# Forgetting attention in a two-layer decoder: half-array products for pairs of heads, a written order for TensorE, gate rows without DMAs, and the output projection begun between the last pairs

## The chip, the cores and the metric

The kernel runs on one core of a Trainium2 chip. A core has TensorE (matrix products into psum banks), VectorE, ScalarE and GpSimd for the element-wise work, and SyncE, whose queue issues the weight loads. The metric is the device time of one execution in microseconds (us); lower is better. Each engine works through its own queue in order, and semaphores order the engines against each other.

## The reference

Two layers on an input of 256 tokens by 1024 channels, float32. Layer 0 mixes tokens by native sparse attention, layer 1 by forgetting attention; each is followed by a squared-ReLU MLP of width 4096, with a norm before and after every part. The change touches layer 1's attention:

```python
def fox_attention(q, k, v, logf):            # q, k, v: [1, 256, 16, 64]
    c = jnp.cumsum(logf, axis=1).transpose(0, 2, 1)
    for i in range(nb):                       # two blocks of 128 queries
        lo, hi = i * blk, (i + 1) * blk
        s = jnp.einsum('bqhd,bkhd->bhqk', q[:, lo:hi], k[:, :hi]) * scale
        s = s + c[:, :, lo:hi, None] - c[:, :, None, :hi]
        causal = jnp.arange(lo, hi)[:, None] >= jnp.arange(hi)[None, :]
        p = jax.nn.softmax(jnp.where(causal, s, NEG_INF), axis=-1)
        outs.append(jnp.einsum('bhqk,bkhd->bqhd', p, v[:, :hi]))

def fox_mixer(h, w_in, b_f, w_out):
    q, k, v, fl = jnp.split(h @ w_in, [1024, 2048, 3072], axis=-1)
    logf = jax.nn.log_sigmoid(fl + b_f)
    return fox_attention(q, k, v, logf).reshape(B, T, 1024) @ w_out
```

## The kernel before, in words

**Precision.** A float32 operand is split into a rounded part `hi` and the rest `lo` (`split`, line 114: ScalarE rounds, VectorE subtracts), and a product is the sum hi·hi + lo·hi + hi·lo: three matmuls (`mm3`, line 148). Weights come in pieces of 128x1024 by `load_w` (line 118) on SyncE's queue and are split in the same way; the tiles for them go round through three pools.

**The planner.** The kernel's text is a program order; a planner reorders each engine's instructions by a cost model, ready work first. `tc.keep_in_program_order` pins an instruction to the written place. Tiles come from pools with a fixed number of buffers; `ps_tile(use)` (line 84) gives one of two psum banks of a use: `m`, `s`, `t`, `o` (2 KB per partition each).

**The forgetting layer.** The value projection makes eight blocks of 128 tokens by 256 columns (line 834), with psum uses listed in `VBANKS`; ScalarE evacuates each to `vf` with the token's norm scale (line 838). `token_scales` (line 822) transposes these scales for use along the free axis. Then come eight pairs of heads (line 915). `project` makes q and k of a pair, transposed (128 channels by 256 tokens): per q or k 8 k-steps of `mm3` into one half of an `m` bank, 24 products of 256 columns each. VectorE scales the result to `full` (line 900). Then `qA`, `kA`, `qB` and `kB` are made of it, per head and per q or k: one rounding and one copy on ScalarE (lines 904, 907) and one subtraction on VectorE (905). They stack hi and lo of a head of 64 channels into operands of 128 rows; `kB` has two more rows, the cumulated log gates, which `gates` (line 910) puts there by two DMAs per pair on ScalarE's queue, against rows of ones in `qB`.

`fox_head` (line 853) then takes one head: per block of 128 queries two products (128 rows, and 66 rows) give the scores over 128 or 256 keys in an `s` bank; VectorE adds the mask and finds the minimum (866; signs are turned), ScalarE takes exp with its sum (869), VectorE scales (870, 872); three transposes (875), ScalarE copies them out (877); then the value products in float32 (878, 879), each as two instructions, which write the head's 64 rows of the pair's `o` bank. `fox_pair` (881) splits that bank into `aT`. The planner mixes all this with the projection of later pairs.

**Around it.** `out_proj` (line 656) multiplies `aT` by the output weights into four accumulators (two banks `m` for tokens 0 to 127, two banks `o` for the rest) by `accumulate` (line 620): eight steps i, `go(i, t)` being six products of 512 columns; the second token block lags for the last `DEFER` steps, so that the norm of the first runs beside it. `mlp` (line 670) calls it and then runs the MLP. At most the planner brings its products forward.

Of the kernel before, what the change touches and what calls it, by code (L numbers as in the profile page):

```python
# [8 lines left out]
F32 = mybir.dt.float32  # L9
# [36 lines left out]
NQT = 2  # L46
KBB = 2
SB_B = 3
FB = 2
AHEAD = 1  # L50
VG = 3
CS = 0
VO = (3, 0, 1, 2)
AG = 2
VBANKS = "mmssoomm"
# [13 lines left out]
def kernel(ctx, tc, x_in, norm_g, w_up, w_down, nsa_w_in, nsa_pos, nsa_w1, nsa_w2,  # L69
# [77 lines left out]

    def mm3(ps, lhs, rhs, start, stop):

        pe.matmul(ps, lhs[0], rhs[0], start=start, stop=False)  # L150
        pe.matmul(ps, lhs[1], rhs[0], start=False, stop=False)  # L151
        pe.matmul(ps, lhs[0], rhs[1], start=False, stop=stop)  # L152
# [467 lines left out]
    def accumulate(acc, steps, done):  # L620
# [17 lines left out]

        for i in range(n):
            yield i  # L640
            if i < n - JMAJ:
                go(i, 0)
# [13 lines left out]
    def out_proj(src, w, layer, after):  # L656
        g = load_g(layer, 1)
        acc = [[ps_tile(c) for _ in range(2)] for c in "mo"]
# [3 lines left out]
        def done(t):  # L662
            add_norm(t, acc[t], g)
            return after(t)

        for _ in accumulate(acc, steps, done):
            pass


    def mlp(layer, src, w_out, after):  # L670
# [18 lines left out]
        out_proj(src, w_out, layer, prep)  # L689
# [94 lines left out]
    mlp(0, aT, nsa_w_out[0], to_fox)  # L784
# [11 lines left out]
    cT = [fx1.tile([H, T], R, name=f"cT{i}") for i in range(2)]  # L796

    qBs = [fx1.tile([DH + 2, 2, T], R, name=f"qB{i}") for i in range(NQT)]
    for q in qBs:
        pool.memset(q[DH:DH + 2].bitcast(F32), 1.0)  # L800

    def logf(t, pf):
        a, e, y, m = (stile(H, n) for n in ("fa", "fe", "fy", "fm"))
        z = stile(H, "fz")
# [15 lines left out]
    rT = [fx1.tile([P, T], F32, name=f"rT{j}") for j in range(2)]  # L820

    def token_scales():

        ps = ps_tile("s")
        for t in range(NT):
            rb = fx.tile([P, T], F32, name="full", bufs=FB)[:, 0:P]
            act.activation(rb, ones, AF.Identity, scale=fox_in[t])
            pe.transpose(ps[:, t * P:(t + 1) * P], rb, ident)
        act.copy(rT[1], ps[:, 0:T])
        act.activation(rT[0], ps[:, 0:T], AF.Identity, scale=-SCALE)  # L830
# [3 lines left out]
    for use, (t, i) in zip(VBANKS, vorder):  # L834
# [7 lines left out]
    token_scales()  # L842

    def cumsum():
# [4 lines left out]
        split(cT[0], cT[1], ps[0:H, 0:T])  # L849

    aT = new_hT()

    def fox_head(h, kA, qA, qB, kB, po):
        rows = slice(h % 2 * DH, (h % 2 + 1) * DH)
        ps = ps_tile("s")
        for t in range(NT):
            ts = slice(t * P, (t + 1) * P)
            o, ks = ps[:, t * T:t * T + (t + 1) * P], slice(0, (t + 1) * P)
            pe.matmul(o, qA[:, h % 2, ts], kA[:, h % 2, ks], start=True, stop=False)
            pe.matmul(o, qB[:, h % 2, ts], kB[:, h % 2, ks], start=False, stop=True)  # L860
        psv = ps.rearrange("p (t k) -> p t k", t=NT)
        sb = fx.tile([P, 3, P], F32, name="s_sb", bufs=SB_B)
        s_sb = [sb[:, 0, :], sb[:, 1:3, :].rearrange("p k c -> p (k c)")]
        mx, sums = stile(2, "mx"), stile(2, "sums")
        for t in range(NT):
            dve.tensor_tensor_reduce(out=s_sb[t], in0=psv[:, t, 0:(t + 1) * P], in1=(caus, mask1)[t], scale=1.0,
                                     scalar=HIGH, op0=OP.add, op1=OP.min, accum_out=mx[:, t:t + 1])
        for t in range(NT):
            act.activation(s_sb[t], s_sb[t], AF.Exp, scale=-1.0, bias=mx[:, t:t + 1], accum_out=sums[:, t:t + 1])
# [114 lines left out]
```

## Time and profile before

| | us |
|---|---|
| median of 3 runs (lowest, highest) | 673.53 (672.61, 674.65) |
| the profiled execution's own time | 675.86 |
| its span, first to last instruction | 673.80 |

| busy in the span | TensorE | VectorE | ScalarE | GpSimd |
|---|---|---|---|---|
| us | 652.9 | 454.3 | 394.8 | 36.9 |

The mean granted clock of TensorE is 0.992 of full speed. A row of the timeline gives the start and the duration of one instruction, or of several of one kind merged (x2). Matmuls are pipelined: a recorded duration reaches past the start of the next one, so the cost of a product is read from start to start. Weight loads (LDWEIGHTS, engine PEld) run beside matmuls. Line numbers are those of the kernel before.

### The profile page before, as it was taken

The page shows a single profiled execution, that of the slowest core. Times are in us where ns is not written, and L with a number is a line of the kernel's source. Part 1 is how long each engine was busy: PE and PEld are TensorE (multiplying, and loading weights), DVE is VectorE, ACT ScalarE, POOL GpSimd, SP SyncE. Part 2 cuts the span into 40 slices and gives each one's busy share as a digit, 9 for nine tenths or more (in the row PEclk, how much of TensorE's full clock was granted, in tenths as well). Part 3 has the DMA queues.
Part 4 walks back from the last instruction along what each step waited for, and adds up shares of the span by engine and source line. Part 5 has one row for each costly group of instructions (what it writes and reads, how often), then busy time and mean ns, then how long its engine had stood idle before and what let it go on. Part 6 is the DMA issues. An engine that isn't in the chain of part 4 may idle for free.

```text
span 673.8 us, 10482 instructions
## 1 busy us (share of the span) xinstructions
PE 652.9 (97%) x3889; PEld 567.2 (84%) x3889; DVE 454.3 (67%) x886; ACT 394.8 (59%) x708; POOL 36.9 (5%) x74
## 2 busy tenths in 40 slices
PE   7999999999999999999999899999999999999996
PEld 6998998988788888888889898887878888888884
DVE  5887898764985656556658677777777475566533
ACT  4868587864865454544547568787676355455321
POOL 1000003212100000000003000000010000000000
PEclk8998999999999999999999999999999999999998
DMA  9666852202696655656636732325476567565301
GB/s 308 174 197 189 232 179 90 64 1 71 200 313 201 220 179 168 213 162 207 192 100 185 226 124 93 95 96 165 156 240 204 158 203 219 151 213 173 119 1 62
DMA packets 74867, 110.20 MB, mean 164 GB/s; under 512 B 4728, under 2 KB 60736, under 8 KB 74816
## 3 DMA queue, kind: packets, MB, share of 16 engines
q1 hardware_dynamic: 72336, 105.48, 50.0%
q10 hardware_dynamic: 2480, 4.06, 1.9%
q8 instruction: 30, 0.49, 0.3%
q14 instruction: 21, 0.17, 0.1%
HBM read 108.44 MB, written 1.05 MB: 162 GB/s over the span
## 4 chain that ended last, share of the span: by engine, by line
PE 78%; DMA 7%; DVE 6%; ACT 5%; issue 3%; POOL 1%; SPq 0%; POOLq 0%; DVEq 0%; ACTq 0%
PE ps_m L716 14%; PE ps_m L717 8%; PE ps_m L150 5%; PE ps_m L152 5%; PE ps_m L151 5%; PE ps_o L150 5%; PE ps_o L151 5%; PE ps_o L152 5%; PE ps_s L150 5%; PE ps_s L152 5%; PE ps_s L151 5%; PE ps_o L562 3%; DMA raw<-in_nsa_w_in_dram 2%; DVE lo L116 2%; PE ps_m L719 2%
## 5 line engine op out<-in xcount | busy, mean ns | idle before, releaser
L116 DVE TENSOR_TENSOR lo<-raw,hi 128x1024 fp32r<-128x1024 f32 (+2 forms) x196 | 237.2, 1214 | 114.6 <-ACT hi L115 108.9
L115 ACT CAST hi<-raw 128x1024 fp32r<-128x1024 f32 (+2 forms) x196 | 203.1, 1043 | 126.4 <-DMA raw<-in_mlp_w_up_dram 43.5
L716 PE MATMUL ps_m<-hT,hi 128*128 128x512 f32 x392 | 140.0, 396 | 0.0
L717 PE MATMUL ps_m<-hT,lo 128*128 128x256 f32 x448 | 116.8, 281 | 0.0
L717 PEld LDWEIGHTS ps_m<-hT,lo 128*128 128x128 f32 x448 | 84.5, 189 | 5.0
L716 PEld LDWEIGHTS ps_m<-hT,hi 128*128 128x128 f32 x392 | 73.6, 188 | 16.1
L151 PE MATMUL ps_m<-hi,hT 128*128 128x256 f32 (+3 forms) x252 | 80.4, 319 | 1.1 <-DVE hT L116 1.1
L152 PE MATMUL ps_m<-lo,hT 128*128 128x256 f32 (+3 forms) x252 | 80.3, 319 | 0.7 <-DVE lo L116 0.7
L150 PE MATMUL ps_m<-hi,hT 128*128 128x256 f32 (+3 forms) x252 | 80.9, 322 | 0.0
L151 PEld LDWEIGHTS ps_m<-hi,hT 128*128 128x128 f32 x252 | 48.5, 192 | 4.5 <-DVE hT L116 2.1
L152 PEld LDWEIGHTS ps_m<-lo,hT 128*128 128x128 f32 x252 | 48.4, 192 | 3.5 <-DVE lo L116 1.1
L150 PEld LDWEIGHTS ps_m<-hi,hT 128*128 128x128 f32 x252 | 48.6, 193 | 2.3
L150 PE MATMUL ps_s<-hi,uh 128*128 128x512 f32 x128 | 50.5, 394 | 0.0
L150 PE MATMUL ps_o<-hi,uh 128*128 128x512 f32 x128 | 50.4, 394 | 0.0
L152 PE MATMUL ps_s<-lo,uh 128*128 128x512 f32 x128 | 50.4, 393 | 0.0
L152 PE MATMUL ps_o<-lo,uh 128*128 128x512 f32 x128 | 50.3, 393 | 0.0
L151 PE MATMUL ps_s<-hi,ul 128*128 128x512 f32 x128 | 50.3, 393 | 0.0
L151 PE MATMUL ps_o<-hi,ul 128*128 128x512 f32 x128 | 50.3, 393 | 0.0
L721 ACT COPY second<-ps_m 128x256 f32<-128x256 f32 x56 | 20.7, 370 | 38.8 <-PE ps_m L719 38.6
L150 PE MATMUL ps_m<-hT,hi 128*128 128x256 f32 x128 | 37.6, 294 | 3.6 <-ACT vf L838 2.3
L152 PE MATMUL ps_m<-hT,hi 128*128 128x256 f32 x128 | 37.2, 291 | 0.0
L151 PE MATMUL ps_m<-hT,lo 128*128 128x256 f32 x128 | 36.4, 284 | 0.0
(242 smaller groups left out, 1126.7 us busy)
## 6 DMA issues: line engine op xcount, KB each, us to landing
raw<-in_mlp_w_up_dram SPq DMA_DIRECT2D x64, 512.0 KB, 3.8
raw<-in_mlp_w_down_dram SPq DMA_DIRECT2D x64, 512.0 KB, 4.1
raw<-in_fox_w_in_dram SPq DMA_DIRECT2D x22, 512.0 KB, 3.7
raw<-in_nsa_w_in_dram SPq DMA_DIRECT2D x18, 512.0 KB, 3.5
raw<-in_nsa_cmp_w_dram SPq DMA_DIRECT2D x8, 512.0 KB, 4.6
raw<-in_nsa_w_out_dram SPq DMA_DIRECT2D x8, 512.0 KB, 4.7
raw<-in_fox_w_out_dram SPq DMA_DIRECT2D x8, 512.0 KB, 3.6
gb<-in_norm_g_dram ACTq DMA_DIRECT2D x7, 512.0 KB, 6.6
```

The costliest lines, as they stand in the source:

```text
L115: act.copy(hi, src)
L116: dve.tensor_tensor(out=lo, in0=src, in1=hi.bitcast(F32), op=OP.subtract)
L150: pe.matmul(ps, lhs[0], rhs[0], start=start, stop=False)
L151: pe.matmul(ps, lhs[1], rhs[0], start=False, stop=False)
L152: pe.matmul(ps, lhs[0], rhs[1], start=False, stop=stop)
L562: pe.matmul(pov[:, hh, br, :], pts[:, j * P:(j + 1) * P], vt[:, kt, br, g, :], start=(kt == 0), stop=(kt == t))
L716: pe.matmul(psv, wh[:, fs], hT[2][:, :, k, :], start=k == 0, stop=False)
L717: pe.matmul(psv[:, 0, :], wl[:, fs], hT[0][:, k, :], start=False, stop=False)
L719: pe.matmul(psv, wh[:, fs], hT[2][:, :, k, :], start=False, stop=True)
L721: act.copy(second, psv[:, 1, :])
```

## The change

Heads 2p and 2p+1 are kept in the upper and lower 64 rows of one `hi` and one `lo` tile (q and k side by side, 128x512): one multiplication by `rT`, one split. Per block of queries a head's scores are four products on 64 rows: hi·hi, hi·lo, lo·hi, and a selector column (`sel`, broadcast over 128) times the cumulated gates (`cX`, which holds their hi and lo for both halves); the two heads alternate, each into an `s` bank of its own. So the gate DMAs, `kB` and `qB` are gone. `turn` transposes both heads of a pair in a row; `values` issues both heads' value products in turn. TensorE's order in this part is pinned as written: between the four quarters of the projection of pair p stand the values of pair p-3, the scores of p-1 and the transposes of p-2. After the last projection the first six steps of the output projection for tokens 0 to 127 (`LEAD`) are written between what is left of the pairs. Accumulators are taken when first used. Two of the value blocks use `s` banks in place of `m`, and `token_scales` stands after the fifth block. Elsewhere the text is as it was. The removed functions are printed above.

```diff
-NQT = 2
-KBB = 2
-SB_B = 3
+SB_B = 4
-AHEAD = 1
-CS = 0
-VBANKS = "mmssoomm"
+VBANKS = "mmssooss"
+PB = 4
+LEAD = 6
...
+    as_traced = [False]
+    def queue(ins):
+        if as_traced[0]:
+            tc.keep_in_program_order(ins)
     def mm3(ps, lhs, rhs, start, stop):
-        pe.matmul(ps, lhs[0], rhs[0], start=start, stop=False)
+        queue(pe.matmul(ps, lhs[0], rhs[0], start=start, stop=False))
...
-    def accumulate(acc, steps, done):
+    def accumulate(acc, steps, done, lead=0):
...
+            if callable(acc[t]):
+                acc[t] = acc[t]()
...
+        for i in range(lead):
+            yield i
+            go(i, 0)
         for i in range(n):
             yield i
-            if i < n - JMAJ:
+            if lead <= i < n - JMAJ:
                 go(i, 0)
...
+    sel = fx1.tile([P, H], R, name="sel")
+    for i in range(4):
+        rows = slice(32 * i, 32 * i + 32)
+        pool.tensor_copy(sel[rows], ident[rows, 32 * i:32 * i + H])
+    cX = fx1.tile([P, T], R, name="cX")
+    pool.memset(cX.bitcast(F32), 0.0)
...
-        split(cT[0], cT[1], ps[0:H, 0:T])
+        c = [cX[32 * i:32 * i + H] for i in range(4)]
+        split(c[0], c[1], ps[0:H, 0:T])
+        for i in range(2):
+            act.copy(c[2 + i], c[i].bitcast(F32))
...
     def project(p, ws):
         fs = slice(p % 2 * P, (p % 2 + 1) * P)
         ps = ps_tile("m")
         for j in range(2):
             for k in range(KD):
                 wh, wl = ws[j][k]
+                mm3(ps[:, j * T:(j + 1) * T], (wh[:, fs], wl[:, fs]), (hT[0][:, k, :], hT[1][:, k, :]), k == 0,
+                    k == KD - 1)
+                if k == KD // 2 - 1 or (j == 0 and k == KD - 1):
+                    yield
+        full = fx.tile([P, 2, T], F32, name="full", bufs=FB)
+        dve.tensor_tensor(out=full, in0=ps.rearrange("p (j t) -> p j t", j=2), in1=rT, op=OP.mult)
+        qk[p] = hi, lo = [fx.tile([P, 2, T], R, name=n) for n in ("qk_hi", "qk_lo")]
+        split(hi, lo, full)
+
+    def scores(p):
+        hi, lo = qk.pop(p)
+        ps = [ps_tile("s") for _ in range(2)]
+        for t in range(NT):
+            ts, ks = slice(t * P, (t + 1) * P), slice(0, (t + 1) * P)
+            for i, (q, k) in enumerate(((hi, hi), (hi, lo), (lo, hi), (None, None))):
+                for hh in range(2):
+                    rows = slice(hh * DH, (hh + 1) * DH)
+                    h = 2 * p + hh
+                    queue(pe.matmul(
+                        ps[hh][:, t * T:t * T + (t + 1) * P],
+                        q[rows, 0, ts] if q else sel[rows, h:h + 1].broadcast_to([DH, P]),
+                        k[rows, 1, ks] if k else cX[rows, ks], start=i == 0, stop=i == 3))
...
+    def values(p):
+        po = ps_tile("o")
+        w = pts.pop(p)
+        for kt in range(2):
             for hh in range(2):
+                queue(pe.matmul(po[hh * DH:(hh + 1) * DH, kt * P:T], vf[:, kt, 2 * p + hh, :],
+                                w[hh][:, T:3 * P] if kt else w[hh][:, 0:T], start=kt == 0, stop=kt == 1))
+        split(aT[0][:, p, :], aT[1][:, p, :], po[:, 0:T])
...
+    as_traced[0] = True
     for p in range(KD):
         if p % 2 == 0:
             ws = load_cols(W, p * P, BW), load_cols(W, 1024 + p * P, BW)
+        parts = project(p, ws)
+        next(parts)
+        if p > 2:
+            values(p - 3)
+        next(parts)
+        if p > 0:
+            scores(p - 1)
+        next(parts)
+        if p > 1:
+            turn(p - 2)
+        finish(parts)
+        if p == 0:
             cumsum()
...
+    next(projection)
+    values(KD - 3)
+    fill(1)
+    scores(KD - 1)
+    fill(1)
+    turn(KD - 2)
+    fill(2)
+    values(KD - 2)
+    fill(1)
+    turn(KD - 1)
+    fill(1)
+    values(KD - 1)
+    as_traced[0] = False
```

## Rows read from the trace of the kernel before

**Rows 1.** The page, its first line and its part 4: the span, and the chain of work that ended last, its shares by engine.
```profile
span 673.8 us, 10482 instructions
...
PE 78%; DMA 7%; DVE 6%; ACT 5%; issue 3%; POOL 1%; SPq 0%; POOLq 0%; DVEq 0%; ACTq 0%
```

**Rows 2.** The windows of the value projection and of the attention: from and to, length, then busy us and instructions of TensorE, its weight loads, VectorE, ScalarE, GpSimd, granted clock, DMA share, GB/s.
```profile
360.00:386.00 26.00, 23.65 (x198) 23.41 (x197) 18.87 (x38) 16.50 (x31) 3.44 (x5) 1.00 0.72 223
386.00:470.00 84.00, 81.94 (x587) 70.84 (x587) 63.03 (x186) 66.39 (x173) 0.00 (x0) 1.00 0.35 110
```

**Rows 3.** TensorE's timeline where the attention begins: start us, duration, engine, line, operation, tiles, shape, count, and in brackets the idle time before it.
```profile
382.03 0.38 PE L828 MATMUL ps_s<-ident,full 128*128 128x128 f32 x2
384.76 0.39 PE L150 MATMUL ps_m<-hT,hi 128*128 128x256 f32 x1 [2.35 <-ACT vf L838]
```

**Rows 4.** ScalarE's timeline in the same stretch.
```profile
383.29 1.04 ACT L115 CAST hi<-raw 128x1024 fp32r<-128x1024 f32 x1 [3.10 <-DMA raw<-in_fox_w_in_dram]
384.24 0.47 ACT L838 ACTIVATE vf<-ps_m,rstd 128x256 f32<-128x256 f32 x1
```

**Rows 5.** TensorE's timeline of one head's scores between projection products.
```profile
407.77 0.28 PE L152 MATMUL ps_m<-hT,hi 128*128 128x256 f32 x1
407.89 0.22 PE L859 MATMUL ps_s<-kA,qA 128*128 128x128 f32 x1
407.95 0.27 PE L860 MATMUL ps_s<-kB,qB 66*128 66x128 f32 x1
408.06 0.33 PE L859 MATMUL ps_s<-kA,qA 128*128 128x256 f32 x1
408.23 0.28 PE L860 MATMUL ps_s<-kB,qB 66*128 66x256 f32 x1
408.35 0.29 PE L150 MATMUL ps_m<-hT,hi 128*128 128x256 f32 x1
```

**Rows 6.** TensorE's timeline of one head's value products between projection products.
```profile
401.32 0.28 PE L151 MATMUL ps_m<-hT,lo 128*128 128x256 f32 x1
401.56 0.65 PE L878 MATMUL ps_o<-pts,vf 128*64 128x256 f32 x2
402.04 0.38 PE L879 MATMUL ps_o<-pts,vf 128*64 128x128 f32 x2
402.35 0.39 PE L152 MATMUL ps_m<-hT,hi 128*128 128x256 f32 x1
402.57 0.28 PE L150 MATMUL ps_m<-hT,hi 128*128 128x256 f32 x1
```

**Rows 7.** TensorE's timeline of the last pair's value products, both heads, between products of the output projection.
```profile
468.41 0.40 PE L152 MATMUL ps_m<-lo,hT 128*128 128x512 f32 x1
468.73 0.66 PE L878 MATMUL ps_o<-pts,vf 128*64 128x256 f32 x4
469.21 0.40 PE L879 MATMUL ps_o<-pts,vf 128*64 128x128 f32 x4
469.54 0.50 PE L150 MATMUL ps_o<-hi,hT 128*128 128x512 f32 x1
469.87 0.39 PE L151 MATMUL ps_o<-hi,hT 128*128 128x512 f32 x1
```

**Rows 8.** TensorE's timeline of a pair whose two heads' value products follow each other directly, the first product of each.
```profile
423.84 0.65 PE L878 MATMUL ps_o<-pts,vf 128*64 128x256 f32 x2
...
424.51 0.65 PE L878 MATMUL ps_o<-pts,vf 128*64 128x256 f32 x2
```

**Rows 9.** TensorE's timeline of one head's three transposes among projection products; the products of lines 152 and 150 that start at 412.58 and 412.92 are left out.
```profile
412.32 0.28 PE L151 MATMUL ps_m<-hT,lo 128*128 128x256 f32 x1
412.53 0.30 PE L875 MATMUL ps_t<-ident,s_sb 128*128 128x128 f32 x1
...
412.79 0.38 PE L875 MATMUL ps_t<-ident,s_sb 128*128 128x128 f32 x2
...
413.13 0.28 PE L151 MATMUL ps_m<-hT,lo 128*128 128x256 f32 x1
```

**Rows 10.** TensorE's timeline of eight transposes in a row, in the layer's second norm.
```profile
482.73 1.03 PE L183 MATMUL ps_t<-ident,h 128*128 128x128 f32 x8
483.52 0.48 PE L150 MATMUL ps_o<-hi,hT 128*128 128x512 f32 x1
```

**Rows 11.** Instruction groups of the attention (386 to 470), TensorE's weight loads for the scores: line, engine, operation, tiles, shape, count | busy us, mean ns | idle before them.
```profile
L859 PEld LDWEIGHTS ps_s<-kA,qA 128*128 128x128 f32 x32 | 6.2, 193 | 0.6 <-DVE kA L905 0.6
L860 PEld LDWEIGHTS ps_s<-kB,qB 66*128 66x128 f32 x32 | 6.1, 191 | 0.2 <-issue 0.2
```

**Rows 12.** TensorE's timeline, its longest idle time in the attention.
```profile
442.42 0.38 PE L150 MATMUL ps_m<-hT,hi 128*128 128x256 f32 x1 [0.66 <-DVE full L900]
```

**Rows 13.** Instruction groups of the attention (386 to 470), as in rows 11.
```profile
L116 DVE TENSOR_TENSOR lo<-raw,hi 128x1024 fp32r<-128x1024 f32 x18 | 21.8, 1223 | 2.7 <-ACT hi L115 2.4
...
L904 ACT CAST qA<-full 64x256 fp32r<-64x256 f32 x16 | 6.5, 404 | 1.6 <-DVE cT L116 0.8 <-DVE full L900 0.7
...
L152 PE MATMUL ps_m<-lo,hT 128*128 128x512 f32 x9 | 3.8, 423 | 0.0
```

**Rows 14.** Instruction groups of the whole kernel, each shape by itself: VectorE and ScalarE on 512 columns.
```profile
L116 DVE TENSOR_TENSOR ul<-u,uh 128x512 fp32r<-128x512 f32 x28 | 19.2, 688 | 6.3 <-ACT uh L115 6.2
L115 ACT CAST uh<-u 128x512 fp32r<-128x512 f32 x28 | 17.4, 622 | 27.3 <-DVE u L697 27.3
```

More of the change, by code (lines that the diff above doesn't have):

```diff
@@ L654, in accumulate, with out_proj @@
         finish(done(1) or ())
-    def out_proj(src, w, layer, after):
+    def out_proj(src, w, layer, after, lead=0):
         g = load_g(layer, 1)
-        acc = [[ps_tile(c) for _ in range(2)] for c in "mo"]
+        acc = [lambda c=c: [ps_tile(c) for _ in range(2)] for c in "mo"]
         steps = [(lambda p=p: load_w(w[p * P:(p + 1) * P, :].unsqueeze(1), 1, D), lambda t, p=p: tok(src, p, t))
@@ L663, in done, with mlp @@
             add_norm(t, acc[t], g)
[L664 to L670, printed above, removed]
+            return after[0](t)
+        yield from accumulate(acc, steps, done, lead)
+    def mlp(layer, projection, prepare, after):
         mctx = ExitStack()
@@ L687, in prep @@
             return gen
-        out_proj(src, w_out, layer, prep)
+        prepare.append(prep)
+        finish(projection)
         g3 = load_g(layer, 3)
@@ L841 @@
             logf(t, ps[:, BW:n])
-    token_scales()
+        if j == VG + 1:
+            token_scales()
     def cumsum():
@@ L896, in project @@
             for k in range(KD):
                 wh, wl = ws[j][k]
-                mm3(ps[:, js], (wh[:, fs], wl[:, fs]), (hT[0][:, k, :], hT[1][:, k, :]), k == 0, k == KD - 1)
-            full = fx.tile([P, T], F32, name="full", bufs=FB)
-            dve.tensor_tensor(out=full, in0=ps[:, js], in1=rT[j], op=OP.mult)
-            for hh in range(2):
-                rows, other = (slice(r * DH, (r + 1) * DH) for r in (hh, 1 - hh))
-                top = (qA, kA)[j]
-                act.copy(top[rows, hh, :], full[rows])
-                dve.tensor_tensor(out=qB[0:DH, hh, :] if j == 0 else kA[other, hh, :], in0=full[rows],
-                                  in1=top[rows, hh, :].bitcast(F32), op=OP.subtract)
-                act.copy(qA[other, hh, :] if j == 0 else kB[0:DH, hh, :], full[rows])
@@ new lines, in turn @@
+    def turn(p):
+        pts[p] = []
+        for sb in sbs.pop(p):
+            pt = ps_tile("t")
+            for k in range(3):
+                queue(pe.transpose(pt[:, k * P:(k + 1) * P], sb[:, k, :], ident))
+            pts[p].append(fx.tile([P, 3 * P], F32, name="pts", bufs=PB))
+            act.copy(pts[p][-1], pt[:, 0:3 * P])
+    def values(p):
+        po = ps_tile("o")
+        w = pts.pop(p)
+        for kt in range(2):
+            for hh in range(2):
+                queue(pe.matmul(po[hh * DH:(hh + 1) * DH, kt * P:T], vf[:, kt, 2 * p + hh, :],
+                                w[hh][:, T:3 * P] if kt else w[hh][:, 0:T], start=kt == 0, stop=kt == 1))
+        split(aT[0][:, p, :], aT[1][:, p, :], po[:, 0:T])
@@ L915 @@
+    qk, sbs, pts = {}, {}, {}
+    as_traced[0] = True
     for p in range(KD):
@@ L917, with fill @@
             ws = load_cols(W, p * P, BW), load_cols(W, 1024 + p * P, BW)
-        waiting.append((p, project(p, ws)))
-        if p == CS:
-            cumsum()
-        if p >= AHEAD:
-            i, kq = waiting.pop(0)
-            gates(i, kq[3])
-            fox_pair(i, *kq)
-    for i, kq in waiting:
-        gates(i, kq[3])
-        fox_pair(i, *kq)
+        parts = project(p, ws)
[10 more added lines that the diff above has]
+        if p == 0:
+            cumsum()
+    prepare = []
+    projection = out_proj(aT, fox_w_out[0], 1, prepare, LEAD)
+    def fill(n):
+        for _ in range(n):
+            next(projection)
+    next(projection)
+    values(KD - 3)
[10 more added lines that the diff above has]
+    as_traced[0] = False
     fox_ctx.close()
-    mlp(1, aT, fox_w_out[0], None)
+    mlp(1, projection, prepare, None)
 _INS = ['x', 'norm_g', 'mlp_w_up', 'mlp_w_down', 'nsa_w_in', 'nsa_cmp_pos', 'nsa_cmp_w1', 'nsa_cmp_w2', 'nsa_w_out',
```

83 lines of the change are left out of this document (27 added, 56 removed).

## The prediction

> **What bounds the kernel now.** I read the page first: the span and the chain that ended last [rows 1]. TensorE carries 78% of that chain, and no other engine more than 7%. So an edit is worth what it takes from TensorE's queue, or from TensorE's waits. Then I read the windows of the two stretches that the change touches [rows 2]: the value projection of the forgetting layer (360 to 386) and its attention (386 to 470). The granted clock is 1.00 in both, the 2.4 GHz level, so no stretch has a clock to win. TensorE is busy for 81.94 of 84 us in the attention, VectorE for 63 and ScalarE for 66: these two bound nothing on average, but they hand over what TensorE reads next. In the other stretch TensorE is idle for 2.35 us, nearly all of it in one place [rows 3]. A busy share hides half of this, since a matmul's recorded end runs past the start of the next one. So I price from start to start in the timeline: a 256-column product costs 0.12 us [rows 5] and a 512-column one 0.23 [rows 7].
>
> **The change part by part.** Sums are against the profiled execution, 675.86 us for a span of 673.8; the median of the three runs is 673.53, 2.3 us less, and I carry the difference over.
>
> *The start, -2.5 us.* The two transposes of the token scales start at 382.03, and at 0.10 us each [rows 10] they leave TensorE free at 382.23. The first q product starts at 384.76 [rows 3]. What it waits for is its psum bank: the last two value blocks use the m banks, and their evacuation (vf, 384.24) stands on ScalarE behind a weight cast that waited for its DMA until 383.29 [rows 4]. The new bank list gives these two blocks the s banks, which are next needed by the first scores, some 9 us later. The weights of pair 0 were loaded before those of the cast at 383.29, so I see nothing else that is late there.
>
> *The value products, -6.0 us.* A head on its own costs TensorE 1.01 us: from 401.32 to 402.57 are 1.25 us, in which two projection steps of 0.12 lie [rows 6]. The last pair shows the two heads issued in turn: four and four products from 468.73 on, and the whole visit costs 469.87 - 468.41 less two steps of 0.23, that is 1.00 [rows 7]. Two heads side by side cost what one costs, since each writes 64 of the array's columns. The change writes this order for all eight pairs. Before: pairs 0, 1, 3 and 6 make two visits each (2.02); in pairs 2, 4 and 5 one head directly follows the other, which adds 0.67 [rows 8] (1.68); pair 7 costs 1.00. Together 8.1 + 5.0 + 1.0 = 14.1. After: 8 x 1.01 = 8.1.
>
> *The scores, +2.4 us.* A head's four products now take 0.46 us, 16 heads 7.4 [rows 5]. After, a pair has sixteen products of 64 rows, eight for each head, alternating between upper and lower half of the array and between two banks. No row of this trace has a product on 64 rows beside another. If they run side by side, as the 64-column ones do [rows 7], a pair takes four short and four long steps, twice 0.46 = 0.92: the same as now. To this comes the change of the array's shape. A visit of value products contains 0.48 us for its two long and so about 0.24 for its two short products [rows 6]; the other 0.3 of the 1.01 is what going into and out of half-array products costs. The scores pay none of that now: 0.12 from the product before and 0.12 to the next [rows 5]. So 1.22 per pair, 9.8 in all. Ends: 0.72 per pair (four steps of 0.06 and four of 0.12 and no price for the shape), -1.6 us; sixteen products one behind another (1.84) and the shape, +9.7. I take the value next to [rows 7], as that row shows half-array products.
> The Trainium skill speaks against this part: "TensorEngine Tiling (Array Packing)", Tiling Modes, Key Properties, says that changing the tiling mode drains TensorE. The 0.3 us of [rows 6] agrees with it. Without that rule the scores would cost nothing and the forecast would be 2.4 us lower.
>
> *The transposes, -1.2 us.* A head's three, scattered among projection products, cost 0.45: from 412.32 to 413.13 are 0.81 us, with three steps of 0.12 in it [rows 9]. Six in a row at 0.10 [rows 10], with 0.1 to get back, are 0.7 per pair, 5.6 in all, against 7.2 if all were scattered. Some were not, so 6.8 before; the ends are -0.4 and -1.6.
>
> *TensorE's waits, -1.5 us.* From 384.76 to 469.54 [rows 3, 7] are 84.8 us. In it are 384 projection products (46.1), 27 products of the output projection (nine on each of three lines [rows 13], 6.2), values 14.1, scores 7.4, transposes 6.8, six of the cumulative sum (0.7): 81.3. The 3.5 left are waits, 2.06 of them visible as idle [rows 2], the longest for full [rows 12], that is for the m bank of the projection. In the written order the bank is two pairs deep and that wait goes. What is late next is the chain from the projection's last product to the next scores: full, hi and lo, 0.69 + 0.62 + 0.69 [rows 14], with the 0.28 that a product's record lasts [rows 6] some 2.3 us. Between lie 24 projection products and a value visit, 3.9 us, so 1.6 are left for what stands ahead of these three in the queues of VectorE and ScalarE. At the end, between pair 7's projection and its scores, lie only a value visit and six output products, 2.4: there I expect a wait of 0.5 to 1. I leave 2.0 in all; the ends are 0 and 5.
>
> *At nothing.* The gate rows came by sixteen DMAs of 2 KB from ScalarE's queue; no instruction is shown waiting for them, so their removal gains nothing and the selector product is priced with the scores. ScalarE loses eight casts of 0.40 per pair [rows 13] and gets one of 0.62 [rows 14]; that is cover for the chain above and no time by itself. The output products only move: 36 stand between the pairs' steps where 27 stood, and 60 follow where 69 did. Layer 0 only gets its accumulators later in the text; its order has no reason to change, and I keep 1 us of spread for the planner.
>
> Sum: -2.5 - 6.0 + 2.4 - 1.2 - 1.5 = -8.8, so 667.1 for a profiled execution and 664.7 for the median.
>
> **The rivals.**
> *The half-row products run one behind another.* For: a load of 66 rows takes as long as one of 128 (191 and 193 ns [rows 11]), and the pair has sixteen loads where it had eight. Against: 64-column products do run two by two: the four of one merged row take 0.66 us in [rows 7], the two of one head 0.65 in [rows 6]. Then the scores cost +9.7 and not +2.4: 672.0, no change that can be seen.
> A page's rule bears on it: "TensorE: Matmul & The Clock Gate", LDWEIGHTS, says that a load's time goes by its columns, not its rows, an estimate of 16 x 107 = 1.7 us per pair. The same page, Packing small matmuls, lets loads of different row groups overlap. The loads of [rows 11] agree with the first; no row here shows the second.
> *Slower: the written order waits for the casts in every pair.* TensorE may no longer step around a late operand. If each of the three steps full, hi, lo finds a weight cast ahead of it (1.22 us on VectorE [rows 13], some 1.0 on ScalarE [rows 4]), the chain is 2.3 + 1.2 + 1.0 + 1.2 = 5.7 against 3.9 of cover: 1.8 per pair and 0.2 to refill, 16 in place of my 2.0, and 678.7. It decides from 1.35 us of wait per pair on. For: VectorE is busy 75% of the time with pieces of that size. Against: both engines lose work, and not every pair meets three casts.
> *The shape costs nothing and nothing waits.* 660.3.
> *The start doesn't move,* because the first projection then waits for its weights: 667.2.
>
> **How the numbers follow.** Forecast 0.60, with its own range of 661 to 668.5; side by side fails 0.13; slower 0.10; all free 0.12; start unmoved 0.05. A measurement here tells about 0.3%, 2.0 us, from no change. So faster 0.60 + 0.12 + 0.05 = 0.77, same 0.13, slower 0.10. The range takes in the free case and the one-behind-another case: 660.0 to 672.5.
>
> **What the profile of the changed kernel would show.** The first q product near 382.3. Eight value visits of four and four products, each 1.0 us. Scores as pairs of starts some 15 ns apart, 1.2 us per pair; if starts are 0.11 apart sixteen times, the first rival holds. A TensorE idle total in the attention below 2 us; idle of over 1 us ahead of each pair's scores, ended by lo or hi, means the slower rival. The stage from 382 to the last value product should be 80.6 us with its 36 output products (87.3 now, less 8.8, and nine more products), and a pair some 8.7. I would be wrong at the root if TensorE's total is that much less and the end still doesn't move: then the second MLP's start hung on something else.

## The result, and the profile after

The changed kernel takes 670.35 us (median) beside 673.96 for the kernel before on the same chip: ratio 0.9935, 95% interval 0.9911 to 0.9959, so 2.8 to 6.0 us less. The forecast was 8.8 us less, 664.7; the range (660.0 to 672.5) holds the time, but only about half of the expected gain came, or less. Run again beside the first experiments it took 671.11 against 674.67, ratio 0.9960 (0.9942 to 0.9979). The ratios leave out disturbed executions, and the first profiled one was such (span 2225 us), so "after" below is the profile of that second run, e0_after.

The page of the kernel after, its span and its chain, answers to [rows 1]:

```profile
span 669.1 us, 10502 instructions
...
PE 77%; DMA 7%; DVE 6%; ACT 5%; issue 3%; POOL 1%; SPq 0%; POOLq 0%; DVEq 0%; ACTq 0%
```

TensorE is still the chain, with 77%. The windows answer to [rows 2]: the attention from the first q product on, and then the output projection with the second MLP's norm. The columns are the stretch, its length, busy time and instructions of PE, PEld, DVE, ACT, POOL, then the granted clock, the DMA share and GB/s:

```profile
380.00:465.00 85.00, 82.58 (x676) 73.61 (x675) 58.10 (x160) 48.84 (x121) 0.00 (x0) 0.98 0.44 136
465.00:500.00 35.00, 33.15 (x162) 26.97 (x162) 26.95 (x40) 23.70 (x41) 2.69 (x4) 1.00 0.57 181
```

VectorE and ScalarE are relieved as planned: 58.10 and 48.84 us of work in 85 us where 63.03 and 66.39 stood in 84 [rows 2]. But TensorE is idle for 2.42 us in the attention and 1.85 us behind it, and the clock of the attention is 0.98, where it was 1.00. The timeline of TensorE, kernel after, shows each part of the change in its place; the first two rows answer to [rows 3], the values to [rows 6, 7], the scores to [rows 5], the transposes to [rows 9]:

```profile
380.71 0.28 PE L156 MATMUL ps_s<-lo,hT 128*128 128x256 f32 x1
380.83 0.28 PE L154 MATMUL ps_m<-hT,hi 128*128 128x256 f32 x1
...
407.00 0.28 PE L156 MATMUL ps_m<-hT,hi 128*128 128x256 f32 x1
407.21 0.87 PE L935 MATMUL ps_o<-pts,vf 128*64 128x256 f32 x8
408.01 0.39 PE L154 MATMUL ps_m<-hT,hi 128*128 128x256 f32 x1
408.23 0.28 PE L155 MATMUL ps_m<-hT,lo 128*128 128x256 f32 x1
...
409.43 0.28 PE L156 MATMUL ps_m<-hT,hi 128*128 128x256 f32 x1
409.64 0.33 PE L898 MATMUL ps_s<-qk_hi 64*128 64x128 f32 x2
...
410.75 0.39 PE L154 MATMUL ps_m<-hT,hi 128*128 128x256 f32 x1
410.97 0.28 PE L155 MATMUL ps_m<-hT,lo 128*128 128x256 f32 x1
...
412.15 0.28 PE L156 MATMUL ps_m<-hT,hi 128*128 128x256 f32 x1
412.27 0.82 PE L925 MATMUL ps_t<-ident,s_sb 128*128 128x128 f32 x6
412.85 0.36 PE L154 MATMUL ps_m<-hT,hi 128*128 128x256 f32 x1
413.05 0.28 PE L155 MATMUL ps_m<-hT,lo 128*128 128x256 f32 x1
```

The first q product (ps_m, L154) follows the last value block (ps_s) without a gap, 24.36 us after the first value block's start (356.47); it was 26.78 before. A value visit costs 408.23 - 407.00 less two steps of 0.12: 0.99 us. The scores' rows are pairs of starts ("x2"), eight of them from 409.64 to 410.75, and cost 410.97 - 409.43 less two steps, 1.30. Six transposes cost 0.66 in the same way. A pair without a wait takes 8.7 us (427.63 to 436.30). These are the forecast's own prices, 1.01, 1.22, 0.7 and 8.7. What is not the forecast's is in the view of TensorE's waits (us in total, times, longest), kernel after, from 380 to 500 us:

```profile
PE ps_s L898 <- DVE qk_lo L114: 1.2, 3, 0.4
PE ps_s L898 <- ACT qk_hi L113: 1.1, 1, 1.1
```

The longest of these stands ahead of pair 1's scores; the view's two other entries are the second MLP's hT, further down. Pair 1's scores in the timeline of TensorE, and the stretch in windows of half a microsecond (same columns as above):

```profile
397.40 0.28 PE L156 MATMUL ps_m<-hT,hi 128*128 128x256 f32 x1
398.77 0.33 PE L898 MATMUL ps_s<-qk_hi 64*128 64x128 f32 x2 [1.09 <-ACT qk_hi L113]
399.50 0.33 PE L898 MATMUL ps_s<-qk_lo,qk_hi 64*128 64x128 f32 x2 [0.40 <-DVE qk_lo L114]
...
401.90 0.41 PE L154 MATMUL ps_m<-hT,hi 128*128 128x256 f32 x1
402.12 0.41 PE L155 MATMUL ps_m<-hT,lo 128*128 128x256 f32 x1
```
```profile
401.00:401.50 0.50, 0.50 (x7) 0.50 (x6) 0.50 (x5) 0.50 (x3) 0.00 (x0) 0.86 1.00 410
401.50:402.00 0.50, 0.50 (x4) 0.50 (x4) 0.34 (x3) 0.50 (x3) 0.00 (x0) 0.50 0.65 246
...
404.50:405.00 0.50, 0.50 (x5) 0.50 (x5) 0.00 (x0) 0.04 (x1) 0.00 (x0) 0.72 0.00 0
```

Between 397.40 and 399.50 TensorE starts only the first two of pair 1's scores. And then, with every operand there, the projection's products start 0.21 us apart where they started 0.12 apart: the granted clock has fallen from 2.4 GHz (1.00) to 1.2 GHz (0.50), from about 401.4 to 404.8, 3.4 us in all. The six transposes in that stretch take 1.14 us in place of 0.57, the 24 products behind them 3.53 in place of 3.04, the six ahead 1.23 in place of 0.72: the fall costs 1.6 us, about as much as the waits ahead of it, and no idle column shows it. Who was late is in the timelines of ScalarE and VectorE (in time order, the last figure in brackets is idle time and who ended it):

```profile
386.32 1.05 ACT L113 CAST hi<-raw 128x1024 fp32r<-128x1024 f32 x1 [1.25 <-DMA raw<-in_fox_w_in_dram]
...
390.76 2.00 ACT L113 CAST hi<-raw 128x1024 fp32r<-128x1024 f32 x2
...
396.22 1.98 ACT L113 CAST hi<-raw 128x1024 fp32r<-128x1024 f32 x2
398.11 0.61 ACT L113 CAST qk_hi<-full 128x512 fp32r<-128x512 f32 x1
```
```profile
387.40 1.23 DVE L114 TENSOR_TENSOR lo<-raw,hi 128x1024 fp32r<-128x1024 f32 x1 [1.44 <-ACT hi L113]
...
391.84 2.36 DVE L114 TENSOR_TENSOR lo<-raw,hi 128x1024 fp32r<-128x1024 f32 x2 [1.23 <-ACT hi L113]
394.12 0.28 DVE L909 CUSTOM_DVE_ANT_0 s_sb<-ps_s,cst 128x128 f32<-128x128 f32 x1
...
397.01 0.68 DVE L884 TENSOR_TENSOR full<-ps_m,rT 128x512 f32<-128x512 f32 x1
397.61 1.22 DVE L114 TENSOR_TENSOR lo<-raw,hi 128x1024 fp32r<-128x1024 f32 x1
398.75 0.69 DVE L114 TENSOR_TENSOR qk_lo<-full,qk_hi 128x512 fp32r<-128x512 f32 x1
```

Pair 0's scores end at 391.7, but its first mask operation stands behind two weight lo's (391.84, 2.36 us) until 394.12; full of pair 1 (397.01) stands behind that softmax, qk_hi (398.11) behind two weight casts (396.22, 1.98 us), and qk_lo (398.75) behind qk_hi and one more lo (397.61). The lateness goes back to an earlier cast (386.32) that had waited 1.25 us for its data: its lo (387.40) stands ahead of pair 0's full, which starts at 388.54, 1.8 us behind the end of pair 0's projection (386.75), and qk_hi (389.26) and the two casts at 390.76 follow that. The second MLP's hT, timelines of TensorE, ScalarE and VectorE:

```profile
486.96 0.51 PE L154 MATMUL ps_m<-hi,hT 128*128 128x512 f32 x1 [0.84 <-ACT hT L113]
488.33 0.50 PE L155 MATMUL ps_m<-hi,hT 128*128 128x512 f32 x1 [0.86 <-DVE hT L114]
```
```profile
484.15 1.05 ACT L113 CAST hi<-raw 128x1024 fp32r<-128x1024 f32 x1 [2.77 <-DMA raw<-in_mlp_w_up_dram]
...
486.35 1.05 ACT L113 CAST hT<-ps_t 128x512 fp32r<-128x512 f32 x2
```
```profile
484.96 2.35 DVE L114 TENSOR_TENSOR lo<-raw,hi 128x1024 fp32r<-128x1024 f32 x2
...
487.60 0.67 DVE L114 TENSOR_TENSOR hT<-ps_t,hT 128x512 fp32r<-128x512 f32 x1
```

hT of the second token block comes to ScalarE behind a weight cast that waited 2.77 us for its data and, between the two, the norm's squares of x (from 485.11 on), which come behind that cast too; and to VectorE behind two weight lo's (2.35 us). In the kernel before the one wait here was 0.37 us (for hT, at 493.84).

From first value block to end of span, in three steps read off the timelines, for before, after and the runs told of below (the end of a visit is the start of the next product; the clock's fall is the time at 0.50, summed over half-microsecond windows, without the last 10 us of the span, where the clock falls in every profile):

| run | to the first q product | on to the end of the last value visit (output products in it) | on to the end of the span | time at the lower clock, where |
|---|---|---|---|---|
| before | 26.78 | 84.8 (27) | 204.3 | none |
| e0_after | 24.36 | 83.9 (36) | 204.4 | 3.4, attention |
| e2_planner_order | 24.36 | 80.6 (36) | 204.4 | none |
| e3_old_banks | 25.15 | 81.5 (36) | 206.0 | 3.4, second norm |
| e1_one_after_other | 24.36 | 86.0 (36) | 204.5 | 3.4, attention |
| f1_same_weights | 24.36 | 79.8 (36) | 203.0 | none |
| f2_more_cover | 24.36 | 79.9 (36) | 204.3 | none |
| f3_before_values_only | 26.64 | 83.5 (37) | 205.3 | 3.4, second norm |
| f4_norm_before_casts | 24.36 | 80.9 (36) | 208.4 | 6.8, second MLP |
| g1_norm_one_cast | 24.36 | 81.5 (36) | 203.7 | none |
| g2_cover_again | 24.36 | 79.6 (36) | 204.3 | none |
| g3_cover_and_norm | 24.36 | 79.4 (36) | 203.9 | none |
| h1_no_written_fill | 24.36 | 77.3 (16) | 210.5 | 3.4, second norm |

What comes ahead of the first value block has the same instruction order on TensorE and VectorE before and after; it takes between 356.3 us (f3) and 359.9 (g1), with time at the lower clock in nine of these 13 profiles (in the kernel before at 11 and at 52 us), which is why I compare these steps and not whole spans.

### The profile page after: what moved, and what is told of

It reads as the page before. It is cut to its first block, busy times and chain, and to the rows that moved or that the text cites. A ratio compares the mean times of both kernels' runs of the same rounds, so it can differ in the third digit from the quotient of the medians.

```text
span 2225.0 us, 10502 instructions
## 1 busy us (share of the span) xinstructions
PE 2217.6 (100%) x3953; PEld 1531.9 (69%) x3953; DVE 457.8 (21%) x854; ACT 384.0 (17%) x654; POOL 35.8 (2%) x77
## 4 chain that ended last, share of the span: by engine, by line
PE 99%; issue 0%; DVE 0%; ACT 0%; POOLq 0%; DVEq 0%; POOL 0%; ACTq 0%
PE ps_m L727 15%; PE ps_m L728 8%; PE ps_m L156 8%; PE ps_m L155 8%; PE ps_m L154 8%; PE ps_o L154 6%; PE ps_o L155 6%; PE ps_o L156 6%; PE ps_s L154 5%; PE ps_s L155 5%; PE ps_s L156 5%; PE ps_o L566 3%; PE ps_m L730 2%; PE ps_s L542 2%; PE ps_t L561 2%; PE ps_s L898 1%
## 5 line engine op out<-in xcount | busy, mean ns | idle before, releaser
L727 PE MATMUL ps_m<-hT,hi 128*128 128x512 f32 x392 | 431.0, 1099 | 0.0
L728 PE MATMUL ps_m<-hT,lo 128*128 128x256 f32 x448 | 292.6, 687 | 0.0
L727 PEld LDWEIGHTS ps_m<-hT,hi 128*128 128x128 f32 x392 | 169.1, 431 | 139.1 <-issue 138.4
L728 PEld LDWEIGHTS ps_m<-hT,lo 128*128 128x128 f32 x448 | 196.3, 438 | 50.1 <-issue 42.0
L155 PE MATMUL ps_m<-hi,hT 128*128 128x256 f32 (+3 forms) x236 | 190.1, 805 | 0.0
L154 PE MATMUL ps_m<-hi,hT 128*128 128x256 f32 (+3 forms) x236 | 188.4, 800 | 0.0
L156 PE MATMUL ps_m<-lo,hT 128*128 128x256 f32 (+3 forms) x236 | 188.2, 797 | 0.0
L154 PE MATMUL ps_o<-hi,uh 128*128 128x512 f32 x128 | 141.0, 1102 | 0.0
L154 PE MATMUL ps_s<-hi,uh 128*128 128x512 f32 x128 | 140.8, 1100 | 0.0
L155 PE MATMUL ps_o<-hi,ul 128*128 128x512 f32 x128 | 140.8, 1100 | 0.0
L154 PEld LDWEIGHTS ps_m<-hi,hT 128*128 128x128 f32 x236 | 121.8, 516 | 25.7 <-issue 23.7
L155 PEld LDWEIGHTS ps_m<-hi,hT 128*128 128x128 f32 x236 | 122.7, 520 | 23.1 <-issue 21.3
```

The lines of the kernel that those rows point to most:

```text
L154: queue(pe.matmul(ps, lhs[0], rhs[0], start=start, stop=False))
L155: queue(pe.matmul(ps, lhs[1], rhs[0], start=False, stop=False))
L156: queue(pe.matmul(ps, lhs[0], rhs[1], start=False, stop=stop))
L727: pe.matmul(psv, wh[:, fs], hT[2][:, :, k, :], start=k == 0, stop=False)
L728: pe.matmul(psv[:, 0, :], wl[:, fs], hT[0][:, k, :], start=False, stop=False)
```

## The experiments

Medians in us and ratios to the kernel before, run beside each set (674.67 for e0 to e3, 674.85 for f1 to f4, 674.38 for g1 to g3, 674.77 for h1):

| run | median | ratio (95% interval) | span |
|---|---|---|---|
| e0_after | 671.11 | 0.9960 (0.9942, 0.9979) | 669.1 |
| e1_one_after_other | 674.14 | 0.9996 (0.9970, 1.0021) | 671.7 |
| e2_planner_order | 669.71 | 0.9943 (0.9920, 0.9966) | 666.3 |
| e3_old_banks | 672.44 | 0.9959 (0.9926, 0.9992) | 669.6 |
| f1_same_weights | 667.35 | 0.9891 (0.9866, 0.9916) | 664.8 |
| f2_more_cover | 667.38 | 0.9897 (0.9867, 0.9927) | 665.2 |
| f3_before_values_only | 672.28 | 0.9963 (0.9946, 0.9979) | 671.7 |
| f4_norm_before_casts | 672.09 | 0.9961 (0.9940, 0.9983) | 671.2 |
| g1_norm_one_cast | 668.49 | 0.9903 (0.9876, 0.9929) | 669.4 |
| g2_cover_again | 668.26 | 0.9902 (0.9878, 0.9926) | 665.5 |
| g3_cover_and_norm | 667.39 | 0.9892 (0.9868, 0.9917) | 664.8 |
| h1_no_written_fill | 671.98 | 0.9965 (0.9945, 0.9985) | 669.9 |

**The first set: the change's own parts.** The change once more, unaltered:

> The changed kernel as it is, for a profile whose rows can be set against those of before. Measured so far: 0.9935 of the time before, a gain of 4.4 us where 8.8 were forecast. Theory W (the written order waits): the scores visit costs about 1.2 us per pair as forecast, and TensorE stands some 0.8 us per pair, or about 6.5 us in all in place of 2.0, mostly ahead of the scores, ended by hi or lo. Theory S (half-row products run one behind another): no such waits, but a scores visit costs 1.7 to 2.1 us. Theory T (tail): the attention is some 9 us shorter to its last value product, and 4 us are given back between there and the second MLP's first accumulation.

One head's four products behind the other's:

```diff
-            for i, (q, k) in enumerate(((hi, hi), (hi, lo), (lo, hi), (None, None))):
-                for hh in range(2):
+            for hh in range(2):
+                for i, (q, k) in enumerate(((hi, hi), (hi, lo), (lo, hi), (None, None))):
```

> The scores' loops are exchanged: within a block of queries all four products of the upper head, then all four of the lower one, so that a product never stands beside one of the other half of the array except at the seam. If alternating heads run side by side now, a pair's scores cost 0.5 to 0.9 us more and the kernel 4 to 7 us: 674 to 677. If they run one behind another already (theory S), nothing changes: within 1 us of the changed kernel.

The order of the text for the heads is not what makes them run side by side. TensorE's timeline, pair 1's scores of this kernel:

```profile
400.73 0.32 PE L898 MATMUL ps_s<-qk_lo,qk_hi 64*128 64x128 f32 x1 [0.76 <-DVE qk_lo L114]
400.74 0.33 PE L898 MATMUL ps_s<-qk_hi 64*128 64x128 f32 x1
400.89 0.27 PE L898 MATMUL ps_s<-qk_hi,qk_lo 64*128 64x128 f32 x1
400.90 0.27 PE L898 MATMUL ps_s<-qk_lo,qk_hi 64*128 64x128 f32 x1
```

The rows come in twos 10 ns apart, one of either head: the second head's first product (400.74, on qk_hi) starts beside the first head's second (400.73, on qk_lo), though all four of the first head are queued ahead of it. A pair's eight starts of two cost 1.17 us there against 1.11. That is 0.5 us over eight pairs. So the time lies where the expectation put it for products that run side by side, but not by the price it named: the other 2.5 us of the 3.0 between the medians, whose intervals overlap, are not explained by it. The profile has longer waits for pair 1's scores (1.64 and 0.76 us) and one of 1.01 for the pts of a value visit (0.13 in e0_after); why they are longer stays open.

Without the pinned order:

```diff
-    as_traced[0] = True
+    as_traced[0] = False
```

> The changed kernel with TensorE's order left to the planner in the pairs and in the gaps (nothing pinned there), all else the same. Theory W: the planner steps around late operands and the kernel gains 2 to 4 us. Theory S or T: the pinned order isn't what costs; no gain, and a loss of 0 to 4 us because transposes and value products are scattered again and half-array visits are split.

The planner keeps the written order but for one output product, and the other engines' queues are the same: the pin does nothing here. So this is a second profile of what is nearly the same program, with another outcome: 80.6 us for the attention, no fall of the clock. In it the weight cast that waited in e0_after started 3.18 us behind the first q product, not 5.49, and TensorE waits 0.5 us for qk_lo in all and never for qk_hi. Two more profiles with the same instruction order up to the last value visit lie between: in f4 that cast starts 3.72 us behind the first q product and the attention takes 80.9, in g1 4.87 and 81.5. So the attention's length goes with when weights land.

The old banks for the value blocks:

```diff
-VBANKS = "mmssooss"
+VBANKS = "mmssoomm"
```

> The changed kernel with the old bank list: the last two value blocks use the m banks again. If the start gained what was forecast, 2.5 us are lost (about 672). If the first projection waits for something else, nothing changes.

The first q product waits 0.63 us for vf and starts 0.8 us later, not 2.5. The cast that this vf stands behind got its data earlier here: it starts 23.7 us after the first value block (380.58 - 356.90) where it started at 25.3 in the kernel before [rows 4] and at 25.9 in e0_after (382.34 - 356.47). The old banks cost what that landing makes late, 0.8 here and 2.3 in f3 below, which has them too. In whole times 0.8 us is not told apart.

**The second set: who holds up TensorE.** The weights of pairs 0 and 1 for all, so that the loads and the casts of the other six pairs' weights are left out:

```diff
-        if p % 2 == 0:
+        if p == 0:
             ws = load_cols(W, p * P, BW), load_cols(W, 1024 + p * P, BW)
```

> The changed kernel, but the q and k weights of pairs 0 and 1 serve all eight pairs: the loads and casts of the weights of pairs 2 to 7 are left out (12 casts of 1.0 us on ScalarE, 12 of 1.2 us on VectorE). TensorE's products are as many as before. Theory A (weight casts queued ahead of full, hi, lo and the softmax make TensorE's waits in the attention): the idle before pair 1's and pair 3's scores goes, the stage from the first q product to the last value product falls from 83.9 to 80-81.5 us, the time by 2.5 to 4 us to about 667.5. Rival B (the pair's own chain full, hi, lo is longer than its cover, casts or not): stage 83 to 84, time 670 to 671.5. Rival C (half-array products are dearer than the quiet pairs show): the same as B, with no idle in the trace.

667.35, and the attention takes 79.8 us. TensorE's waits in it, profile of this kernel:

```profile
PE ps_s L898 <- DVE qk_lo L114: 0.4, 1, 0.4
```

The one that is left stands ahead of pair 7's scores, at the tail, where the forecast had named one. Theory A holds: with the casts gone the pair's own chain fits its cover. B and C had 670 and more.

More cover in the written order, all work kept:

```diff
         next(parts)
+        next(parts)
         if p > 2:
             values(p - 3)
-        next(parts)
-        if p > 0:
-            scores(p - 1)
-        next(parts)
-        if p > 1:
-            turn(p - 2)
         finish(parts)
+        if p > 1:
+            turn(p - 2)
+        if p > 0:
+            scores(p - 1)
```

> The changed kernel with another written order in a pair: the values after three quarters of the projection, and transposes and then scores behind all of it. From the last projection product of a pair to its scores stand now 48 products, a value visit and six transposes, some 7.5 us, where 24 products and a visit, 3.9 us, stood; the softmax gets a whole pair too. Theory A and rival B both: the waits for hi and lo inside the loop go (but not those of the last pair, whose tail is unchanged), stage 81 to 82 in place of 83.9, time -2 to -3 us. Rival C: no change, 671. A new wait would be full or the softmax arriving late for the transposes; then 671 to 673.

667.38, as fast as without the casts. TensorE's waits in the profile of this kernel, and its window:

```profile
PE ps_m L155 <- DVE hT L114: 1.1, 1, 1.1
PE ps_m L154 <- ACT hT L113: 0.6, 1, 0.6
PE ps_t L925 <- DVE s_sb L916: 0.3, 1, 0.3
```
```profile
381.00:461.00 80.00, 79.61 (x669) 70.79 (x667) 55.94 (x156) 48.74 (x119) 0.00 (x0) 1.00 0.43 139
```

No wait for qk_hi or qk_lo is left, TensorE is busy for 79.61 of 80 us, and the clock stays at 1.00, though the weight cast compared under e2 starts 4.45 us behind the first q product here, later than e2's 3.18. The casts may stand where they do, as long as what waits for them isn't needed so soon.

One part alone, on the kernel before (`fox_head` now returns its `pts` and the products stand in `fox_pair`):

```diff
+        w = [fox_head(2 * p + hh, *kq, po) for hh in range(2)]
+        for kt in range(2):
+            for hh in (1, 0):
+                i = pe.matmul(po[hh * DH:(hh + 1) * DH, kt * P:T], vf[:, kt, 2 * p + hh, :],
+                              w[hh][:, T:3 * P] if kt else w[hh][:, 0:T], start=kt == 0, stop=kt == 1)
+                tc.keep_in_program_order(i)
```

> The kernel before, with one part of the change alone: the value products of the two heads of a pair issued in turn as one visit of four, in all eight pairs. By the price of the prediction, 14.1 us of visits become 8.1: -6 us, 668 if nothing else comes late. Rival: the visit must now wait for the second head's weights in place of the first's, and the planner places the rest differently, so that a part of it comes back as waits: 670 to 672. If the visits cost what they did: 674.

The rival's mechanism, at a price just above its range. Like for like (ten output products more, 0.23 us each) the attention falls from 84.8 to 81.2, 3.6 us; TensorE's waits in this profile:

```profile
PE ps_m L150 <- DVE full L903: 2.3, 5, 0.5
...
PE ps_t L875 <- DVE s_sb L872: 1.4, 6, 0.4
```

The waits for full and for the softmax are 2.3 and 1.4 us where the kernel before had 1.1 and 0.4: 2.2 of the 6 us come back at once as waits, all of them for results of VectorE. Then the waits for hT are 1.7 where 0.37 was, and behind them the clock falls for 3.4 us. So the value products alone don't bring their 6 us; the waits for full and for the softmax are not there in e0_after, where VectorE and ScalarE have less to do.

The second norm's hT ahead of the weight casts (`norm_first` makes `split` pin both its instructions):

```diff
+            norm_first[0] = layer == 1 and b == NAT
             ws = load_cols(w_up[layer], b * BW, BW)
+            norm_first[0] = False
...
-            return gen
+            return hT_first(gen) if layer == 1 and t == 1 else gen
```

> The changed kernel, with one thing pinned: on ScalarE and VectorE the second token block's hT of the second MLP comes ahead of the casts of the weights for the MLP's next blocks (in the changed kernel six of each stand ahead of it). Theory A, applied to the stretch behind the attention: the two waits for hT there, 0.84 and 0.86 us, go to some 0.4 in all (0.37 in the kernel before), time -1 to -1.5 us. Rival: the casts are then late for the next blocks and TensorE waits there instead: same time or +1 to 3 us.

The rival. The waits for hT are gone and the time is no better than the change's; TensorE's waits behind the attention, this kernel:

```profile
PE ps_t L763 <- DVE u L718: 1.0, 1, 1.0
PE ps_m L740 <- DVE lo L114: 0.8, 1, 0.8
PE ps_o L164 <- ACT uh L113: 0.5, 1, 0.5
```

2.3 us in three places where casts are now late, and 6.8 us at the lower clock.

**The third set: a cure behind the attention.** Only the last of the six casts, the second half of `load_cols` for the same block, comes behind hT (`last_late` is set for that block alone, and hT is pinned as in f4):

```diff
-            hi, lo = load_w(wv[:, k:k + m, c0:c0 + n], m, n, later)
+            norm_first[0] = last_late[0] and k > 0
+            hi, lo = load_w(wv[:, k:k + m, c0:c0 + n], m, n, later)
+            norm_first[0] = False
```

> The changed kernel, with one weight load pinned in place of all: of the six casts on either engine that stand ahead of the second token block's hT in the second MLP, only the last, whose data lands last, comes behind it. Theory A for this stretch (a cast that waits for its DMA holds up hT): the two waits for hT, 0.84 and 0.86 us, become 0.3 to 0.6 in all, and unlike with all six pinned no cast is late behind it; time -1 to -1.5 us, 669.5 to 670. Rival: hT is late by its own chain (norm, transposes), the waits stay above 1.2 us, time unchanged at 671; or the cast is late for the next block: slower.

One wait of 1.49 us for hT is left where two of 0.84 and 0.86 were: above the 1.2 us that I set as the rival's sign, so by the wait the rival is right. VectorE still has two weight lo's (2.35 us) ahead of hT. The median is 2.6 us under e0_after's, more than this accounts for; the two were not run side by side.

> The order of f2_more_cover once more, unchanged, beside its successor on the same chip: 667 to 668 by f2's own median, 3 to 4 us under the changed kernel.

> The order of f2_more_cover and the one late cast of g1 together. The two waits are in different stretches, so by theory A their gains add: f2's 667.4 less 1 to 1.5 us, 666. If hT is late by its own chain: 667.4.

f2's order again gives 668.26, and with g1's cast 667.39, ratio 0.9892. The two differ by less than the intervals: the profile has 0.4 to 0.5 us less behind the attention (203.9 against 204.3 twice), which is all that can be claimed. g3 and f2 are the fastest versions here, some 7 us under the kernel before and 3 to 4 under the changed one.

**Last, the output products not written into the gaps:** `next(projection)` and the calls of `fill` taken out.

> The changed kernel, with the output products no longer written between the last pairs' steps: the planner alone puts some of them there, fewer than the 36 of the changed kernel, and six transposes of the last pair come right behind a value visit. Theory (the output products in the gaps are worth what they cover): pair 7's softmax, from its scores to its transposes, stands uncovered for 1.5 to 3 us, so the time is 672.5 to 674; the waits behind the attention for hT stay, since as many products stand between the last output product and them. Rival (a product in a gap is only one fewer behind it): the products that are not in gaps cover the second MLP's norm and its weights' DMAs instead, the hT waits fall to the 0.37 us of the kernel before, and the time stays at 670 to 671.5.

Neither. The planner puts 16 of the 36 there by itself. TensorE waits nowhere over 0.2 us for the last pair's softmax, so the theory's uncovered wait isn't there; the waits for hT stay (0.7 and 1.0 us), so the rival's isn't either. With 20 products at 0.23 us moved back the attention would be 81.9, 1.3 above e2's, and the rest 205.9. That is 1.5 above e0_after's 204.4, as in e3 (206.0): what a fall of the clock costs, once more. By these stages, where the output products stand is worth about 1 us; in whole times (0.9965 against e0_after's 0.9960) it isn't told apart.

## Why the prediction was wrong in size

*Start, -2.5: right.* 2.4 in every run with the new banks, and e3 shows the cast of [rows 4] as its cause.

*Value products, scores, transposes, -4.8 together: right.* With 0.99, 1.30 and 0.66 us a pair they come to 23.6 us where the forecast had 23.5. The first rival (sixteen products one behind another) is out: 1.11 us, not 1.84. The prices of the trace of before held for a shape that it didn't contain. The Trainium skill, in "TensorE: Matmul & The Clock Gate", Packing small matmuls, lets loads of different row groups overlap. This trace agrees: weight loads of the kernel after in one pair's scores (count, total us, mean ns) are four kinds of four, 0.19 us each, and all sixteen, 3.0 us, lie in a visit of 1.3:

```profile
L898 PEld LDWEIGHTS ps_s<-qk_lo,qk_hi 64*128 64x128 f32 x4 | 0.4, 187 | 0.0
...
L898 PEld LDWEIGHTS ps_s<-qk_hi 64*128 64x128 f32 x4 | 0.4, 185 | 0.1
```

*TensorE's waits, "I leave 2.0 in all; the ends are 0 and 5": the step that failed.* Work without waits is 78.6 us by these prices (384 and 36 products, values, scores, transposes, cumulative sum). The attention takes 79.8 without the weights' casts, 80.6 in e2, where the forecast's 2.0 are met, and 83.9 in e0_after, 5.3 us of waits: from start to start 1.8 at pair 1's scores, 0.65 each at pair 3's and pair 7's, 0.6 at the values of pair 5, and 1.6 for the clock. Two things are in that sum that were not in the working. The casts ahead of full, hi and lo are not spread evenly: they come in twos when the weights of the next two pairs land, and pair 0's softmax stood behind them too, which the working had not asked for. This is the slower rival's mechanism, in pairs 1 and 3 and not in all; the waits of pairs 5 and 7 are there without the casts too, in f1. And a wait was priced at its own length. The prediction said of the clock that "no stretch has a clock to win"; it did not ask what it has to lose. 1.6 us of e0_after's 5.3 are the clock's fall behind the wait.

*"The output products only move", at nothing: wrong by 2.1.* From the last value visit to the end there are nine output products fewer, 2.05 us, and yet it takes 204.4 us where 204.3 were. 1.3 of the 2.1 are the waits for hT behind weight casts. Another 0.5 lies spread evenly over the last 813 products, the same in both kernels: from their first start to the end of the span are 170.84 us in e0_after and 170.33 before, and the other changed kernels come to 170.8 to 171.4 (f3, which is the kernel before but for one part, to 170.2). Why they are slower stays open, and 0.3 I could not place. f3 shows the same waits in the order of the kernel before, and h1 shows them with 20 products more ahead, so it isn't the number of products; f4 shows that the casts are what hT stands behind, and that moving all of them costs more than it gives.

So of 8.8 us, 6.5 are there in a profile in which the weights land early (e2: 2.42 + 4.2 - 0.1) and 3.2 in one in which they land late (e0_after: 2.42 + 0.9 - 0.1), where the forecast had 2.5 + 4.2 + 2.1. The median gain, 3.6 to 4.4 us in the two settings of the changed kernel and 5.0 in e2, lies between. How often the clock falls in the attention of the executions that were not profiled can't be seen. Their mean granted clock can: e0_after's nine go from 0.996 (669.57 us) to 0.987 (674.31), and as 3.4 us at half the clock take 0.0026 of the mean, the slowest has, by estimate, some three falls more than the fastest, at places that the record doesn't show. f1's six lie within 1.2 us, with clocks of 0.993 to 0.996.

## What to carry to other kernels

Time taken from the engine that bounds is given back where the next engine's queue has its lumps: for each operand that the bounding engine will now want sooner, list what stands ahead of it on its maker's queue, bulk casts first, and write the order so that a lump more fits between making and use. f2 did this with no work removed and got as much as leaving the casts out. Price a wait of TensorE by what its clock does behind it, too: here two waits of 1.5 us together cost as much again in clock, and like ones elsewhere cost none.

## What the runs showed of the hardware

Two things that I had not expected. TensorE starts products of the upper and the lower 64 rows side by side even when those of one head are queued behind each other (e1, 10 ns apart), at nearly the price of the alternating order; so for TensorE "in order", as the text on the chip has it, is too strict. In these rows it didn't go past a product that waits: the second head's first product had its operand, qk_hi, and still started only with the first head's second (400.73, behind the 0.76 us for qk_lo). And from the first value block on the granted clock fell to 1.2 GHz in six of these profiles, for 3.4 us (f4: 6.8), each time behind two or three hold-ups close together (e0_after: 1.09 and 0.40 us; f3: 0.60 and 1.11; h1: 0.68 and 1.02). But f2 (0.62 and 1.09), g2 (0.92 and 0.78) and e0_after's own second place (0.84 and 0.86) show like waits and no fall, so the waits alone don't settle it.
